# Output weights of the first attention split in the token-major stage, and the last HGRN unit's modulation sums in the places of the HGRN weights

## The chip, the cores and the metric

The kernel runs on one core of a Trainium2 chip, as one launch. The metric is the device time of that launch in microseconds. Everything is computed in float32: TensorE gets each large operand as two parts, a rounded high part and the rest (`hi`, `lo`, here called a split), and multiplies three times (hi·hi, hi·lo, lo·hi).

## The reference

A two-layer diffusion trunk over 1024 latent tokens and 256 context tokens of width 1024. What the change touches lies in layer 0, the even layer. Cut to that:

```
def even_mixer(h_lat, h_ctx, w_in, w_out, ...):
    aq, ak, av, bq, bff, bfb, bi, bg = split(h @ w_in)      # for latent and context tokens
    oa = gqa_axial_attention(...)                            # 8 query heads, 2 key heads
    ob = hgrn2_bidirectional(...)                            # 4 heads, chunked scans both ways
    y  = concat([oa, rms_norm(ob) * silu(bg)]) @ w_out       # 1024 x 1024 output weights
...
mod = silu(c) @ w_mod[l] + b_mod[l]                          # shift, scale, gate for each of two places
x = x + g1 * rms_norm(y, norm_post_mix[l])
```

`w_out` is read from `even_w_out`; `mod` comes from `w_mod`, and its three groups of 2048 columns are summed one after another during layer 0. Neither depends on the tokens' path, so the kernel can place that work where it likes, as long as it is done before its use.

## The kernel before

**Stages.** `even_mixer` first runs `even_token_major`: it normalises and modulates ten tiles of 128 tokens, and multiplies them by the columns of `w_in` for keys and values (kind 0, 256 columns), HGRN inputs (kind 1, 512 columns) and queries (kind 2, 512 columns). A table `plan` lists the products in order, and with each a list of small pieces of other work (`items`: the three pieces K of a key tile, the pieces Q of a query tile, I for the copy-out of an input tile, N for a norm, T and M for transposes and modulation, W for splitting a weight). A product has eight steps of three matmuls; after step k the items with index up to n(k+1)/8 of the list of n are issued. Items are therefore spread evenly, and a longer list moves each of its items to an earlier step. TensorE, ScalarE, VectorE and GpSimd run in exactly this written order (`in_order`); the DMA queue of SyncE (SP) is put in order by the framework's scheduler, with some loads chained among themselves.

Then `hgrn` runs 12 units (4 heads x 3 segments: 256 context tokens, then 512 and 512 latent ones). `chain(u)` is unit u's decay ladder: seven levels m = 1, 2, 4 ... 64, in which VectorE multiplies `hK`, `hQ` and `hT`, ScalarE copies `hKM` (up to m = 16), and TensorE forms small blocks (`h_pd`, from m = 16 on `h_pa`). Between the levels the loop issues matmuls of the next unit's projection (`fill`), the previous unit's end (`side`), one step of the modulation sums (`mods`), and one step of `out_weight`.

**Output weights.** `out_weight(m)`, once in each of the units 3 to 10, loads a 128x1024 piece of `even_w_out` into place `r1`, copies its high part to `r2` on ScalarE (`w_oh`), subtracts on GpSimd (`w_o`), and stores both to the scratch tensor `wod`. In the attention `load_w` fetches the pairs back; the first four go into the weight places `v0h` ... `v3l`, which the HGRN projection has left by then.

**Modulation sums.** `mod_sums` for group 2 runs during the last unit, in which no projection is left to fill TensorE. Each of its eight steps multiplies 128 rows of `w_mod` (two tiles `m_raw`, 512 KB each) into one bank `g_ps`. Its places are `r1`, `r2` and four homes `K2_ij` of the attention's keys, in a pool that begins only where `xh` and `xl`, the projection's inputs, end. Each step reuses the places in turn: six places, so three steps ahead. `begin()` closes the pool of `xh`, opens the attention's pool and starts the attention's first loads; it is called ahead of the last unit.

Of the kernel before, what the change touches and what calls it, by code (L numbers as in the profile page):

```python
# [20 lines left out]
P = 128  # L21
# [47 lines left out]
class Trunk:  # L69
# [148 lines left out]
    def mod_load(self, l, g, k):  # L218
        raws = []
        for i in range(2):  # L220
            of = self.m_tags[self.m_next % len(self.m_tags)]
            raw = of() if callable(of) else self.wp.tile([P, 1024], F32, name="m_raw", tag=of)
            self.m_next += 1
            c0 = 2048 * g + 1024 * i
            self.nc.sync.dma_start(raw, self.a["w_mod"][l, k * P:(k + 1) * P, c0:c0 + 1024])
            raws.append(raw)
        return raws
# [31 lines left out]
            if k == KT - 1:  # L259
                self.mod_finish(l, g, rows, tp, sp)  # L260

    def mod_sums(self, groups, gp, tp, sp, homes):


        self.m_next = 0
        def gate(l, g):
            sl, gi = (slice(64, 128), 1) if 2 * g + 1 == 5 else (slice(0, 64), 0)
            t = sp.tile([P, 2, 512], F32, name="gate_bw", tag="hF", bufs=2)
            self.nc.sync.dma_start(t[sl, 0], self.a["gate_b"][l, gi])
            self.nc.sync.dma_start(t[sl, 1], self.a["gate_w"][l, gi])  # L270
            return t[:, 0], t[:, 1]

        self.m_tags = ["r1", "r2"] + homes
        steps = [(l, g, k) for l, g in groups for k in range(KT)]
# [242 lines left out]
    def even_token_major(self, xh, xl, gps, tp, mp, rp, sp, hg):  # L517
# [149 lines left out]
        with self.in_order(*self.compute):  # L667
# [52 lines left out]
            X_ = [lambda t=t: load_x(t) for t in range(NT)]  # L720
            plan = [(0, 3, [K[0], K[1], K[0], W_[3]]),
                    (1, 0, [W_[4], X_[7], K[1], K[2], W_[5], X_[8], K[0], X_[9], K[2], N[4], K[3]]),
                    (1, 1, [K[1], K[3], N[5], K[2], I[0], N[6], K[3], N[7]]),
# [10 lines left out]
                    (2, 2, [Q[1], Q[0], Q[0], H[1], Q[1]])]  # L734
            plan += [(2, t, [Q[t - 1], Q[t - 2], Q[t - 2]] + [Q[t - 1]]) for t in range(3, 8)]
            plan += [(2, 8, [Q[7], Q[6], Q[6], H[2], Q[7]]), (2, 9, [Q[8], Q[7], Q[7], Q[8]])]
            for i, t, items in plan:
                def hook(k):
                    n = len(items)
                    for f in items[n * k // KT:n * (k + 1) // KT]:  # L740
                        if f:
                            f()
                product(i, t, range(KT), hook)
# [14 lines left out]
    def hgrn(self, xh, xl, gp):  # L758
# [212 lines left out]
                outs = [o for o in outs if next(o, "end") != "end"]  # L971
                yield

        w_out = a["even_w_out"].rearrange("(k p) n -> p k n", p=P)

        def out_weight(m):

            k = 2 * (m % 4)
            raw = self.wp.tile([P, 1024], F32R, name="w_o", tag="r1")
            nc.sync.dma_start(raw.bitcast(F32).rearrange("p (a b) -> p a b", a=2), w_out[:, k:k + 2, 512 * (m // 4):512 * (m // 4) + 512])  # L980
            yield
            yield
            yield
            hi = self.wp.tile([P, 1024], F32R, name="w_oh", tag="r2")
            nc.scalar.copy(hi, raw.bitcast(F32))
            yield
            nc.gpsimd.tensor_tensor(out=raw, in0=raw.bitcast(F32), in1=hi.bitcast(F32), op=OP.subtract)
            yield
            for i, t in enumerate((hi, raw)):
                nc.sync.dma_start(self.wod[m, i].bitcast(F32), t.bitcast(F32))  # L990

        tails = []

        def side():
# [3 lines left out]
        with self.in_order(*self.compute):  # L998
            prepare(3)
            next(mods, None)  # L1000
            for _ in first:
                pass


            for u in range(len(units)):
                last = u + 1 == len(units)
                fill = iter(()) if last else project(u + 1)
                weight = out_weight(u - 3) if 3 <= u < 11 else iter(())
                if last:
                    att, homes = begin()  # L1010
                    next(att)
                    mods = self.mod_sums([(0, 2)], gp, tp, sp, homes)
                    next(mods)
                if u < 8:
                    with self.in_order(mybir.EngineType.SP, behind=True):
                        self.odd_bias_scratch(u)
                x = 0
                for _ in chain(u):
                    side()
                    next(weight, None)  # L1020
                    if x % 3 or last:
                        next(mods, None)
                    for _ in range(3):
                        next(fill, None)
                    side()
                    x += 1
                x = 0
                for _ in fill:
                    x += 1
                    if x % 2 == 0:  # L1030
                        side()
            x = 0
# [75 lines left out]
    def even_attention(self, gp, tp, pp1, sp, more):  # L1108
# [25 lines left out]
        def load_w(m):  # L1134
            pool, tag = (self.wp, f"v{m}") if m < 4 else (more["wp"], f"w{m}")
            W[m] = [pool.tile([P, 1024], F32R, name="w_" + x, tag=tag + x) for x in "hl"]
            for i, t in enumerate(W[m]):
                nc.sync.dma_start(t.bitcast(F32), self.wod[m, i].bitcast(F32))
# [189 lines left out]
        def step(n):  # L1328

            for _ in range(n):  # L1330
# [3 lines left out]
                elif late:  # L1334
# [10 lines left out]
        load_q(2)  # L1345
        load_ctx_keys(1)
        yield
        later = [lambda m=m: load_w(m) for m in range(4)] + [lambda: load_keys(0, 0), lambda: load_keys(0, 1),
                 lambda: load_values(0, NT - 2), lambda: load_keys(1, 0), lambda: load_keys(1, 1)]
        for s in range(N + 8):  # L1350
            pair, half = s // 2, s % 2
            if s < N:
# [1437 lines left out]
    def even_mixer(self):  # L2790
        nc, a, pool = self.nc, self.a, self.pool
        with ExitStack() as es:
# [20 lines left out]
            with ExitStack() as e2:  # L2813
                self.m_tags, self.g_tag = ("r1", "r2"), "hKM"
                sp = pool(e2, "hg", 2, side="right")
                pp = pool(e2, "hg_psum", 1, space=PSUM)
                mods = self.mod_bursts([(0, 1)], tp, sp)

                def begin():
                    eh.close()  # L2820
                    at = self.at = Homes(pool(es, "at0", 2), None, ("l_p", "a_ph1", "a_pl1", "gate", "y"))
                    homes = [lambda t=f"K2_{i}{j}": at.first.tile([P, 1024], F32, name="m_raw", tag=t, bufs=1)
                             for i in range(2) for j in range(2)]
                    return self.even_attention(gp, tp, pp, at, more), homes
# [139 lines left out]

# [6 lines left out]
```

## Time and profile before

| what | us |
|---|---|
| median of 3 runs (lowest, highest) | 3281.98 (3278.56, 3282.49) |
| the profiled execution | 3279.68 |
| its span | 3277.6 |
| DVE busy, POOL busy in the span | 2159.5, 1592.6 |
| first and last copy `w_oh` on ScalarE | 340.0, 567.2 |
| first and last modulation matmul of the last unit | 592.2, 617.8 |

The span runs from the first to the last recorded instruction; the profiled execution lasted 2.1 us longer than its span and was 2.3 us shorter than the median. PE is TensorE, PEld its weight loads, ACT ScalarE, DVE VectorE, POOL GpSimd, SP or SPq the DMA queue that SyncE issues. A row of the timeline gives start, duration, engine, line, operation, output and inputs, and in brackets the time for which the engine had sat idle before it and what ended that. A row of the waits gives the sum, the number of times, and the longest. A row of stretches gives busy times by engine, the clock that TensorE was granted, and the DMA engines' busy share and GB/s.

### The profile page before, as it was taken

To read this page: it belongs to the slowest core of one execution; us is meant where nothing else is said; L and a number is where in the kernel's file an instruction comes from. 1 tells how busy PE (TensorE), PEld (TensorE's weight loads), DVE (VectorE), ACT (ScalarE), POOL (GpSimd) and SP (SyncE) were. 2 spreads that over 40 slices of the span, in tenths; PEclk is the share of its full clock that TensorE was granted. 3 is DMA by queue.
4 is the path that set the end of the run, shared out by engine and by line. 5 is a ranking of instruction groups with operands and counts; after the bars stand their busy time and mean duration, and the time that the engine had idled before them with its cause. 6 is when DMAs were issued, how large, how long until landed. Compare 5 with 4: busy or idle time off the path is not lost.

```text
span 3277.6 us, 48744 instructions
## 1 busy us (share of the span) xinstructions
PE 3076.2 (94%) x18161; PEld 2545.1 (78%) x18161; DVE 2159.5 (66%) x3603; ACT 1506.7 (46%) x2697; POOL 1592.6 (49%) x1173
## 2 busy tenths in 40 slices
PE   7989999789998899999999989999998989999999
PEld 4867777578886688888888768899986758888787
DVE  4456666577775788888678662477775465555687
ACT  3323333366665434433444442566665543343444
POOL 1130222287774677777500111677775367777300
PEclk8999999899999899999999989999998989999999
DMA  7333222621114244443375672222224212222755
GB/s 252 105 102 112 87 89 75 229 87 63 58 48 162 82 152 147 142 145 137 137 249 200 226 227 107 74 63 62 61 73 162 91 64 84 77 88 84 249 193 189
DMA packets 214709, 412.91 MB, mean 126 GB/s; under 512 B 25392, under 2 KB 87360, under 8 KB 214472
## 3 DMA queue, kind: packets, MB, share of 16 engines
q1 hardware_dynamic: 204776, 376.24, 34.2%
q0 software_dynamic: 9696, 33.57, 2.6%
q8 instruction: 142, 2.33, 0.3%
q14 instruction: 95, 0.78, 0.1%
HBM read 322.67 MB, written 87.44 MB: 125 GB/s over the span
## 4 chain that ended last, share of the span: by engine, by line
PE 76%; DVE 12%; DMA 4%; ACT 3%; issue 3%; POOL 2%; SPq 0%; POOLq 0%; ACTq 0%; DVEq 0%
PE g_ps L140 21%; PE u_g L140 13%; PE d_ps L140 11%; PE u_v L140 10%; PE u_pc L140 3%; PE a_pv L140 2%; PE c_pv L140 2%; PE c_s L140 2%; PE c_pt L2593 2%; PE a_pt L1210 2%; DMA m_raw<-in_w_mod 1%; DVE a_pl L1212 1%; PE o_ps L140 1%; PE a_s L140 1%; DMA d_rawB<-in_w_down 1%
## 5 line engine op out<-in xcount | busy, mean ns | idle before, releaser
L148 POOL TENSOR_TENSOR rs_r<-rs_e,mhalf 128x1 f32<-128x1 f32 (+3 forms) x102 | 82.4, 809 | 788.3 <-DVE rs_e L147 370.3
L140 PE MATMUL d_ps<-d_Bl,d_Ah 128*128 128x512 f32 x704 | 277.3, 394 | 3.4 <-DVE d_Bl L1976 2.9
L140 PE MATMUL d_ps<-d_Bh,d_Ah 128*128 128x512 f32 x704 | 276.6, 393 | 3.8 <-ACT d_Bh L1975 2.0
L2576 POOL TENSOR_SCALAR c_p<-c_p,rl 128x640 f32<-128x640 f32 (+1 forms) x128 | 232.8, 1820 | 94.2 <-DVE rl L2575 62.4
L140 PE MATMUL d_ps<-d_Bh,d_Al 128*128 128x512 f32 x704 | 276.2, 392 | 0.7 <-DVE d_Al L1976 0.6
L140 PE MATMUL g_ps<-xh,w_hi 128*128 128x512 f32 (+1 forms) x640 | 259.7, 406 | 5.6 <-DVE hq L805 3.5
L1190 POOL TENSOR_SCALAR l_p<-l_p,rl 128x1280 f32<-128x1280 f32 x64 | 225.4, 3521 | 54.9 <-DVE rl L1189 49.0
L140 PE MATMUL g_ps<-xh,w_lo 128*128 128x512 f32 (+1 forms) x640 | 240.2, 375 | 1.6 <-POOL w_lo L2476 1.6
L140 PE MATMUL g_ps<-xl,w_hi 128*128 128x512 f32 (+1 forms) x640 | 240.4, 376 | 0.0
L1212 DVE TENSOR_TENSOR a_pl<-a_pt,a_ph 128x512 fp32r<-128x512 f32 (+1 forms) x200 | 118.9, 602 | 87.0 <-ACT a_ph L1211 86.6
L366 DVE CUSTOM_DVE_ANT_0 m_raw<-m_raw,c_row 128x512 f32<-128x512 f32 x128 | 149.7, 1180 | 24.9 <-DMA m_raw<-in_w_mod 24.6
L1651 DVE TENSOR_TENSOR f_u<-u_v,f_p 128x512 f32<-128x512 f32 x88 | 60.4, 687 | 158.8 <-PE u_v L140 158.8
L140 PEld LDWEIGHTS d_ps<-d_Bl,d_Ah 128*128 128x128 f32 x704 | 133.2, 189 | 34.8 <-DVE d_Bl L1976 6.8
L140 PEld LDWEIGHTS d_ps<-d_Bh,d_Ah 128*128 128x128 f32 x704 | 133.3, 189 | 33.7 <-ACT d_Bh L1975 3.6
L1637 POOL TENSOR_TENSOR w_S4l<-w_s,w_S4h 128x512 fp32r<-128x512 f32 x44 | 57.1, 1298 | 208.2 <-ACT w_S4h L1636 208.2
L140 PEld LDWEIGHTS d_ps<-d_Bh,d_Al 128*128 128x128 f32 x704 | 133.4, 189 | 29.3 <-DVE d_Al L1976 1.7
L1211 ACT CAST a_ph<-a_pt 128x512 fp32r<-128x512 f32 (+1 forms) x200 | 101.8, 517 | 109.1 <-PE a_pt L1210 109.1
L2596 DVE TENSOR_TENSOR c_pl<-c_pt,c_ph 128x256 fp32r<-128x256 f32 (+1 forms) x256 | 112.9, 469 | 58.5 <-ACT c_ph L2595 57.3
L140 PE MATMUL g_ps<-w_hi,xh 128*128 128x512 f32 (+1 forms) x368 | 142.8, 388 | 5.5 <-DVE xh L2350 2.9
L140 PEld LDWEIGHTS g_ps<-xh,w_hi 128*128 128x128 f32 x640 | 123.8, 193 | 25.0 <-issue 7.6
L140 PEld LDWEIGHTS g_ps<-xh,w_lo 128*128 128x128 f32 x640 | 123.3, 193 | 24.7 <-POOL w_lo L2476 2.0
L140 PE MATMUL g_ps<-w_lo,xh 128*128 128x512 f32 (+1 forms) x368 | 137.6, 374 | 4.0 <-DVE w_lo L2337 2.9
(602 smaller groups left out, 10026.3 us busy)
## 6 DMA issues: line engine op xcount, KB each, us to landing
w_raw<-in_w_up SPq DMA_DIRECT2D x88, 512.0 KB
d_rawA<-actd SPq DMA_DIRECT2D x77, 512.0 KB
d_rawB<-in_w_down SPq DMA_DIRECT2D x74, 512.0 KB
m_raw<-in_w_mod SPq DMA_DIRECT2D x128, 256.0 KB
m_raw<-in_w_mod SPq DMA_DIRECT2D x48, 512.0 KB
actd<-f_t SPq DMA_DIRECT2D x22, 640.0 KB
actd<-f_t SPq DMA_DIRECT2D x22, 512.0 KB
vcd<-cv_st POOLq DMA_DIRECT2D x20, 512.0 KB, 2.9
```

Source lines behind the costliest of these rows:

```text
L140: return self.nc.tensor.matmul(out, lhsT, rhs, start=start, stop=stop, skip_group_check=True, **k)
L148: nc.gpsimd.tensor_tensor(out=r[:p, :n], in0=e[:p, :n], in1=self.mhalf[:p, :n], op=OP.pow)
L366: nc.vector.tensor_tensor_reduce(out=w, in0=w, in1=halves[1][n % 2], scale=1.0, scalar=0.0, op0=OP.mult, op1=OP.add, accum_out=acc[:, k, o ...
L1190: nc.gpsimd.tensor_scalar(Pt[:, :nk], Pt[:, :nk], rl, None, op0=OP.mult)
L1210: nc.tensor.transpose(pt[:, m, qt * P:(qt + 1) * P], Pt[:, kts[j + m] * P:(kts[j + m] + 1) * P], self.ident)
L1211: nc.scalar.copy(ph[:, j:j + n], pt[:, :n])
L1212: nc.vector.tensor_tensor(out=pl[:, j:j + n], in0=pt[:, :n], in1=ph[:, j:j + n].bitcast(F32), op=OP.subtract)
L1637: nc.gpsimd.tensor_tensor(out=lo, in0=part(j, name), in1=hi.bitcast(F32), op=OP.subtract)
L1651: nc.vector.tensor_tensor(out=out, in0=x, in1=y, op=OP.add)
L2576: nc.gpsimd.tensor_scalar(Pt[:, :n], Pt[:, :n], rl, None, op0=OP.mult)
L2593: nc.tensor.transpose(pt[:, j, :], Pt[:, (src + j) * P:(src + j + 1) * P], self.ident)
L2596: nc.vector.tensor_tensor(out=vap(pl, o, dims), in0=pt[:, :cnt], in1=vap(ph, o, dims).bitcast(F32), op=OP.subtract)
```

## The change

- Each product from plan entry 3 on gets extra items: `out_load(m)` loads a 128x512 piece (256 KB) of `even_w_out` into the low place of one of three new pairs `o0` to `o2`, `out_split(m)`, two entries later, copies the high part on ScalarE and subtracts in place on VectorE, and `out_store(m)` stores both halves to `wod`. There are 16 pieces. `out_weight` in the HGRN loop is gone.
- `mod_sums` takes as places `r1`, `r2` and the eight weight places `v0h` ... `v3l`: ten, so five steps ahead. The homes in the attention's pool are gone.
- `begin()` is called after the third level of the last unit, with the sums already going.
- The attention's deferred loads `later` fetch keys and values first, and the four pairs of output weights after them.
- The scratch for the descriptors of GpSimd's DMAs is halved.

```diff
-        self.m_tags = ["r1", "r2"] + homes
+        self.m_tags = ["r1", "r2"] + [f"v{i}{x}" for i in range(4) for x in "hl"]
...
+            def out_load(m):
+                k, c0 = m % 8, 512 * (m // 8)
+                O[m] = [self.wb.tile([P, 512], F32R, name="w_o" + x, tag=f"o{m % 3}{x}") for x in "hl"]
+                with self.chained():
+                    nc.sync.dma_start(O[m][1].bitcast(F32), w_out[:, k, c0:c0 + 512])
+
+            def out_split(m):
+                hi, lo = O[m]
+                nc.scalar.copy(hi, lo.bitcast(F32))
+                nc.vector.tensor_tensor(out=lo, in0=lo.bitcast(F32), in1=hi.bitcast(F32), op=OP.subtract)
+
+            def out_store(m):
+                c = 512 * (m % 2)
+                for i, t in enumerate(O.pop(m)):
+                    nc.sync.dma_start(self.wod[m // 2, i][:, c:c + 512].bitcast(F32), t.bitcast(F32))
...
+            for m in range(16):
+                at = 3 + 3 * m // 4
+                plan[at][2].append(lambda m=m: out_load(m))
+                plan[at + 2][2].extend((lambda m=m: out_split(m), lambda m=m: out_store(m)))
...
-        def out_weight(m):
...
-            nc.scalar.copy(hi, raw.bitcast(F32))
-            yield
-            nc.gpsimd.tensor_tensor(out=raw, in0=raw.bitcast(F32), in1=hi.bitcast(F32), op=OP.subtract)
...
                 if last:
-                    att, homes = begin()
-                    next(att)
-                    mods = self.mod_sums([(0, 2)], gp, tp, sp, homes)
+                    mods = self.mod_sums([(0, 2)], gp, tp, sp)
                     next(mods)
...
                     x += 1
+                    if last and x == 3:
+                        att = begin()
+                        next(att)
...
-        later = [lambda m=m: load_w(m) for m in range(4)] + [lambda: load_keys(0, 0), ...
+        later = [lambda: load_keys(0, 0), ... + [lambda m=m: load_w(m) for m in range(4)]
...
-    nc = bacc.Bacc("TRN2", target_bir_lowering=False, num_devices=1, dynamic_dma_scratch_size=8192)
+    nc = bacc.Bacc("TRN2", target_bir_lowering=False, num_devices=1, dynamic_dma_scratch_size=4096)
```

VectorE in the token-major stage, around the products (0, 4) to (0, 6), before: the norm of a token tile (`n_x`), the value part of a key tile (`v_st`) and its rotation (`qk_n` to `qk_r`) follow one another directly.

```order
L147 TENSOR_SCALAR rs_e<-ms 128x1
L615 TENSOR_SCALAR n_x<-n_x,rs_r 128x1024
L527 TENSOR_TENSOR v_st<-g_ps,v_st 128x2x64
L454 TENSOR_REDUCE qk_ms<-qk_sq 128x2
L147 TENSOR_SCALAR rs_e<-qk_ms 128x2
L147 TENSOR_SCALAR rs_e<-ms 128x1
L615 TENSOR_SCALAR n_x<-n_x,rs_r 128x1024
L459 TENSOR_TENSOR qk_n<-g_ps,rs_r 128x128
```

The same place of VectorE after the change; `w_ol` is the low half of a piece of the output weights.

```order
L147 TENSOR_SCALAR rs_e<-ms 128x1
L614 TENSOR_SCALAR n_x<-n_x,rs_r 128x1024
L731 TENSOR_TENSOR w_ol<-w_ol,w_oh 128x512 x2
L526 TENSOR_TENSOR v_st<-g_ps,v_st 128x2x64
L453 TENSOR_REDUCE qk_ms<-qk_sq 128x2
L147 TENSOR_SCALAR rs_e<-qk_ms 128x2
L147 TENSOR_SCALAR rs_e<-ms 128x1
L614 TENSOR_SCALAR n_x<-n_x,rs_r 128x1024
L731 TENSOR_TENSOR w_ol<-w_ol,w_oh 128x512
L458 TENSOR_TENSOR qk_n<-g_ps,rs_r 128x128
```

Three subtractions now stand ahead of the rotation of this key tile, two of them ahead of its value part.

GpSimd in the HGRN units 4 and 5, before: the subtraction `w_o` stands between the unit's outputs (`h_o`, stored to `hgd`) and the copy `hqb`.

```order
L148 TENSOR_TENSOR rs_r<-rs_e,mhalf 128x2
L1096 TENSOR_SCALAR h_dg<-ident,rs_r 128x128 x2
L1103 TENSOR_TENSOR h_o<-h_o,hgate 128x256
L1105 DMA hgd<-h_o 128x256
L987 TENSOR_TENSOR w_o<-w_o,w_oh 128x1024
L934 COPY hqb<-hQ 128x512
L987 TENSOR_TENSOR w_o<-w_o,w_oh 128x1024
L148 TENSOR_TENSOR rs_r<-rs_e,mhalf 128x4
```

The same place after.

```order
L148 TENSOR_TENSOR rs_r<-rs_e,mhalf 128x2
L1098 TENSOR_SCALAR h_dg<-ident,rs_r 128x128 x2
L1105 TENSOR_TENSOR h_o<-h_o,hgate 128x256
L1107 DMA hgd<-h_o 128x256
L955 COPY hqb<-hQ 128x512
L148 TENSOR_TENSOR rs_r<-rs_e,mhalf 128x4
```

All eight such subtractions have left GpSimd.

The DMA queue of SP around the last unit, before: `w_h` and `w_l` are fetched output weights, `K_`, `V_` and `a_q` the attention's keys, values and queries.

```order
L1138 DMA w_h<-wod 128x1024
L1144 DMA K_0c<-k2d 128x2x256
L1124 DMA a_q<-q2d 128x256 x2
L1156 DMA V_8_5947<-v2d 128x2x256
L1124 DMA a_q<-q2d 128x256
L1144 DMA K_1c<-k2d 128x2x256
L225 DMA m_raw<-in_w_mod 128x1024 x14
L1138 DMA w_l<-wod 128x1024
L1150 DMA K_00_6373<-k2d 128x1024
```

The same place after; two more `m_raw`, for `r1` and `r2`, stand far ahead of these rows, at the HGRN unit 4.

```order
L224 DMA m_raw<-in_w_mod 128x1024 x3
L268 DMA gate_bw<-in_gate_b 64x512
L269 DMA gate_bw<-in_gate_w 64x512
L224 DMA m_raw<-in_w_mod 128x1024 x11
L1146 DMA K_0c<-k2d 128x2x256
L1126 DMA a_q<-q2d 128x256 x2
L1158 DMA V_8_6131<-v2d 128x2x256
L1126 DMA a_q<-q2d 128x256
L1146 DMA K_1c<-k2d 128x2x256
L1152 DMA K_00_6323<-k2d 128x1024
```

Before, 14 of the 16 modulation tiles are asked for after everything else that the last unit and the attention's first block need; after, all are asked for ahead of that, and the fetches of the output weights have moved behind the keys.

More of the change, by code (lines that the diff above doesn't have):

```diff
@@ L220, in mod_load @@
         for i in range(2):
-            of = self.m_tags[self.m_next % len(self.m_tags)]
-            raw = of() if callable(of) else self.wp.tile([P, 1024], F32, name="m_raw", tag=of)
+            raw = self.wp.tile([P, 1024], F32, name="m_raw", tag=self.m_tags[self.m_next % len(self.m_tags)])
             self.m_next += 1
@@ L260, in mod_bursts, with mod_sums @@
                 self.mod_finish(l, g, rows, tp, sp)
-    def mod_sums(self, groups, gp, tp, sp, homes):
+    def mod_sums(self, groups, gp, tp, sp):
         self.m_next = 0
@@ L720, in even_token_major @@
             X_ = [lambda t=t: load_x(t) for t in range(NT)]
+            w_out, O = a["even_w_out"].rearrange("(k p) n -> p k n", p=P), {}
+            def out_load(m):
[11 more added lines that the diff above has]
+                    nc.sync.dma_start(self.wod[m // 2, i][:, c:c + 512].bitcast(F32), t.bitcast(F32))
             plan = [(0, 3, [K[0], K[1], K[0], W_[3]]),
@@ L972, in tail @@
                 yield
-        w_out = a["even_w_out"].rearrange("(k p) n -> p k n", p=P)
-        def out_weight(m):
-            k = 2 * (m % 4)
-            raw = self.wp.tile([P, 1024], F32R, name="w_o", tag="r1")
-            nc.sync.dma_start(raw.bitcast(F32).rearrange("p (a b) -> p a b", a=2), w_out[:, k:k + 2, 512 * (m // 4):512 * (m // 4) + 512])
-            yield
-            yield
-            yield
-            hi = self.wp.tile([P, 1024], F32R, name="w_oh", tag="r2")
-            nc.scalar.copy(hi, raw.bitcast(F32))
[L986 to L990, printed above, removed]
         tails = []
@@ L1007, in hgrn @@
                 fill = iter(()) if last else project(u + 1)
-                weight = out_weight(u - 3) if 3 <= u < 11 else iter(())
                 if last:
-                    att, homes = begin()
-                    next(att)
-                    mods = self.mod_sums([(0, 2)], gp, tp, sp, homes)
+                    mods = self.mod_sums([(0, 2)], gp, tp, sp)
                     next(mods)
@@ L1019, in hgrn @@
                     side()
-                    next(weight, None)
                     if x % 3 or last:
@@ L1347, in even_attention @@
         yield
-        later = [lambda m=m: load_w(m) for m in range(4)] + [lambda: load_keys(0, 0), lambda: load_keys(0, 1),
-                 lambda: load_values(0, NT - 2), lambda: load_keys(1, 0), lambda: load_keys(1, 1)]
+        later = [lambda: load_keys(0, 0), lambda: load_keys(0, 1), lambda: load_values(0, NT - 2), lambda: load_keys(1, 0),
+                 lambda: load_keys(1, 1)] + [lambda m=m: load_w(m) for m in range(4)]
         for s in range(N + 8):
@@ L2821, in begin @@
                     at = self.at = Homes(pool(es, "at0", 2), None, ("l_p", "a_ph1", "a_pl1", "gate", "y"))
-                    homes = [lambda t=f"K2_{i}{j}": at.first.tile([P, 1024], F32, name="m_raw", tag=t, bufs=1)
-                             for i in range(2) for j in range(2)]
-                    return self.even_attention(gp, tp, pp, at, more), homes
+                    return self.even_attention(gp, tp, pp, at, more)
                 try:
```

## The prediction

> **What bounds the kernel now.** I read the page first (span, busy shares, the chain that ended last), then stretches by stage, then TensorE's waits in each stage, then timelines around those waits.
>
> ```profile
> span 3277.6 us, 48744 instructions
> PE 76%; DVE 12%; DMA 4%; ACT 3%; issue 3%; POOL 2%; SPq 0%; POOLq 0%; ACTq 0%; DVEq 0%
> 70.00:222.00 152.00, 138.89 (x734) 114.33 (x734) 84.64 (x161) 53.73 (x94) 43.91 (x32) 1.00 0.33 101
> 222.00:592.00 370.00, 344.97 (x3823) 274.61 (x3824) 241.98 (x483) 115.64 (x212) 70.65 (x74) 0.97 0.30 100
> 592.00:622.00 30.00, 22.23 (x332) 9.83 (x330) 17.81 (x36) 5.35 (x9) 0.00 (x0) 0.89 0.94 350
> ```
>
> Three quarters of the chain is TensorE (PE), so a wait of PE is time, and what runs beside a busy PE is free. The stretches (PE, PEld, DVE, ACT, POOL, then clock, DMA share, GB/s) are the token-major stage once its products run, the HGRN units up to the last projection, and the last unit with its modulation sums. Only the third is bound by the DMA engines (share 0.94), and PE has most to gain per microsecond there. PE's waits, in the second and the third stretch:
>
> ```profile
> PE h_pa L140 <- DVE hQ L891: 11.1, 6, 2.4
> ...
> PE g_ps L140 <- DMA m_raw<-in_w_mod: 6.9, 7, 5.2
> ```
>
> **HGRN units: eight GpSimd subtractions leave.** The first of those waits is no weakness of the ladder itself:
>
> ```profile
> 372.97 0.68 DVE L891 TENSOR_TENSOR hQ<-hQ,hT 128x512 f32<-128x512 f32 x1
> 375.67 3.40 DVE L891 TENSOR_TENSOR hQ<-hQ,hT 128x512 f32<-128x512 f32 x1
> 376.14 2.36 POOL L987 TENSOR_TENSOR w_o<-w_o,w_oh 128x1024 fp32r<-128x1024 f32 x1
> 379.21 0.46 PE L140 MATMUL h_pa<-hQ,hKM 128*32 128x32 f32 x32 [2.43 <-DVE hQ L891]
> 408.23 2.84 DVE L891 TENSOR_TENSOR hQ<-hQ,hT 128x512 f32<-128x512 f32 x1
> 411.22 0.46 PE L140 MATMUL h_pa<-hQ,hKM 128*32 128x32 f32 x32 [2.34 <-DVE hQ L891]
> 574.01 0.46 PE L140 MATMUL h_pa<-hQ,hKM 128*32 128x32 f32 x32 [1.41 <-DVE hQ L891]
> 347.54 2.57 POOL L987 TENSOR_TENSOR w_o<-w_o,w_oh 128x1024 fp32r<-128x1024 f32 x1
> 347.89 2.25 DVE L892 TENSOR_TENSOR hT<-hT 128x16 f32<-128x16 f32 x1
> ```
>
> The same VectorE instruction takes 0.68 us alone and 3.40 or 2.84 us beside the GpSimd subtraction `w_o`, and then PE waits. Five of the eight subtractions end in such a wait: two like 379.21, two like 411.22, and 574.01. The sixth wait in the row is the rest (11.1 - 2 x 2.43 - 2 x 2.34 - 1.41 = 0.15 us). In the three units of 256 tokens the slowed one is a small `hT` (row 347.89), while PE has the next projection of 512 tokens to do, and no wait follows. Without `w_o`, hQ ends 3.40 - 0.68 = 2.72 us earlier (all of a 2.43 wait goes) or 2.84 - 0.68 = 2.16 us earlier (2.16 of 2.34 go), and in the last case all of 1.41: 2 x 2.43 + 2 x 2.16 + 1.41 = **10.6 us gained**. What is late next is `hKM` on ScalarE, which loses the copy `w_oh` from its queue as well. Above, the gain is bounded by the whole row, 11.1; below, I put half, 5, if the ladder meets PE again one level later. I take 10.6.
>
> [...]
>
> **Last unit: modulation tiles come earlier.** Now:
>
> ```profile
> 593.58 16.55 SPq L225 DMA_DIRECT2D m_raw<-in_w_mod  x14
> 595.00:600.00 5.00, 0.25 (x2) 0.19 (x4) 1.57 (x3) 0.77 (x2) 0.00 (x0) 0.64 1.02 365
> 599.75 2.35 PE L140 MATMUL g_ps<-m_raw,csil 128*32 128x512 f32 x6 [5.22 <-DMA m_raw<-in_w_mod]
> 593.75 0.68 DVE L889 TENSOR_TENSOR hK<-hK,hF 128x512 f32<-128x512 f32 x1
> 603.40 0.69 DVE L891 TENSOR_TENSOR hQ<-hQ,hT 128x512 f32<-128x512 f32 x1 [6.73 <-PE h_pd L140]
> 605.27 0.68 DVE L891 TENSOR_TENSOR hQ<-hQ,hT 128x512 f32<-128x512 f32 x1
> 615.48 0.69 DVE L889 TENSOR_TENSOR hK<-hK,hT 128x512 f32<-128x512 f32 x1 [1.38 <-PE h_pa L140]
> 618.29 1.09 PE L908 MATMUL h_kt<-ident,hK 128*128 128x128 f32 x8
> ```
>
> All tiles but two are issued at 593.58 or later, when `xh` is given up. PE waits 5.22 us for the second step, and after it runs at the pace of the loads (1 MB a step at 365 GB/s and more: 2.5 to 2.9 us). Since the ladder's blocks stand behind the sums in PE's order, VectorE waits too (6.73 us). The ladder goes from its first `hK` (593.75) to its last (615.48) in 21.73 us, six level steps. After the change, the first five steps' ten tiles have places before the unit's first sum. These are the places that the output weights used, and the queue filled them here, as PE let them go, between
>
> ```profile
> 565.94 0.33 SPq L1138 DMA_DIRECT2D w_h<-wod  x1
> 590.29 0.32 SPq L1138 DMA_DIRECT2D w_h<-wod  x1
> ```
>
> so the tiles are asked for then. The last three steps follow as the first three free their places. Then nothing but VectorE, ScalarE and PE in turn sets the pace: 605.27 - 603.40 = 1.87 us a level where the data was there. The last two levels have PE between hK and hQ (row 615.48 waited for it); I add 0.25 for each and get 6 x 1.87 + 2 x 0.25 = 11.7 instead of 21.73 us: **10.0 us gained**. The transposes `h_kt` (618.29) follow the ladder by the same distance. Bounds: 6.9, PE's DMA waits alone, and 10.5, without the 0.25. What moved behind the tiles is not needed so soon:
>
> ```profile
> L140 PE MATMUL g_ps<-K_0c,a_q x16: 278/365/1202, 622.4 to 641.2; 128*128 128x256 f32 x16
> L140 PE MATMUL a_s<-K,a_q x256: 387/397/501, 656.6 to 982.7; 128*128 128x512 f32 x128
> L140 PE MATMUL g_ps<-w_h,a_oh x160: 393/478/483, 690.7 to 1036.9; 128*128 128x512 f32 x160
> ```
>
> The first keys are used at 622.4, some 612 after the gain. They are issued once the third step has freed its place, near 600, and the output weights have until about 680. If that cover were gone, each 512 KB of the four pairs would cost 1.4 us.
>
> **Token-major stage: what comes in.** 16 loads, 16 copies, 16 subtractions, 32 stores. Prices, from equal or equally wide instructions:
>
> ```profile
> 77.57 0.69 DVE L631 TENSOR_TENSOR xl<-n_t,xh 128x512 fp32r<-128x512 f32 x1
> 108.91 0.59 ACT L571 COPY b_st<-g_ps 128x512 f32<-128x512 f32 x1
> 97.08 0.43 DVE L487 TENSOR_TENSOR qk_r<-qk,qk 128x256 f32<-128x256 f32 x1 [0.35 <-POOL qk L483]
> 98.53 0.38 PE L537 MATMUL k_pt<-ident,qk_r 128*128 128x128 f32 x2
> 104.03 0.43 DVE L487 TENSOR_TENSOR qk_r<-qk,qk 128x256 f32<-128x256 f32 x1 [0.35 <-POOL qk L483]
> 104.93 0.38 PE L537 MATMUL k_pt<-ident,qk_r 128*128 128x128 f32 x2
> 139.01 0.41 PE L537 MATMUL k_pt<-ident,qk_r 128*128 128x128 f32 x2 [0.63 <-DVE qk_r L475]
> 75.93 0.33 PE L623 MATMUL n_pt<-ident,n_x 128*128 128x128 f32 x1 [1.90 <-DVE n_x L615]
> 1150.16 5.43 SPq L351 DMA_DIRECT2D m_raw<-in_w_mod  x4
> 1152.62 0.90 DVE L366 CUSTOM_DVE_ANT_0 m_raw<-m_raw,c_row 128x512 f32<-128x512 f32 x1 [0.79 <-DMA m_raw<-in_w_mod]
> ```
>
> All on the path they would cost 16 x (0.69 + 0.59) = 20.5 us; the stretch has room (VectorE 84.64 of 152 us, ScalarE 53.73), so most is hidden behind PE's products. What isn't are transposes in PE's order whose input now comes later. Key tile 4: its rotation ends at 97.51, its transposes start at 98.53, 1.0 us of slack; three subtractions stand ahead (1.9 us, as VectorE starts one every 0.62): 0.9 us. Key tile 6: slack 0.5 us, again three subtractions since (1.9), its transposes two steps earlier in a longer list (2 x 0.7), less the 0.9 by which PE is late already: 1.9. The transposes of tiles 4 to 7, which already wait 1.90 us for `n_x`, are asked for one step earlier: 0.7. Context transposes that wait for one of three banks, their copies on ScalarE being behind: between 0 and 2, I take 1. The wait at 139.01 goes (-0.6). Sum: **4 us lost**. Below, the bound is -0.6, all else hidden; above, 20.5.
>
> The pieces themselves come in time: a 256 KB load can be used 1152.62 - 1150.16 = 2.5 us after its issue. A place goes round in store 2.5, load 2.5, copy 0.6, subtraction 0.7, some queueing: about 7 us for three pieces, and 13 pieces after the first three want 30 us of the 50 in which they run. The SP queue is held by stores that wait for the two engines; behind them stand the last two `w_in` loads, needed some 5 us after their landing. The other edits (scratch halved, loads in another order) cost nothing while GpSimd's DMAs are as few as here.
>
> **Sum.** 3279.7 for the profiled execution - 10.6 - 10.0 + 4 = 3263.1; the median of the runs lies 2.3 higher, so **3265 us**. A change under 0.2% (6.6 us) can't be told from none in this kernel.
>
> **Rivals.**
> - [...] Chance 0.16.
> - The last unit gains only 4, as a tile still comes late or the first softmax, bound by other engines, gives time back: 3271. For it: SP takes its queue in order, and `gate_bw` stands among the tiles. Chance 0.12.
> - The change doesn't do what it says to the ladder: hQ is late for another reason (the copies of hKM), and 5 of 10.6 come: 3271. Against it: row 372.97. Chance 0.06.
> - Slower: the places' round trip becomes the stage's pace. The 13 pieces are 4.3 rounds; it decides where a round takes over (50 + 21) / 4.3 = 16.5 us, 2.4 times what the rows give. At 19 us the rounds take 82, 32 more than the 50, in place of the 4: 3265 - 4 + 32 = 3293. For it: every piece needs two trips and an in-order queue. Chance 0.04.
> - My forecast, 3260 to 3270: 0.62.
>
> Faster by over 0.2% (under 3275.4) are the forecast, most of the first rival and all of the next two: 0.62 + 0.10 + 0.12 + 0.05 = 0.89, of which I take 0.03 off for what I haven't seen: 0.86. Same 0.10, slower 0.04. The range reaches from the forecast with all upper bounds, 3259, to the first rival's middle and a little more, 3275.
>
> **What would show it.** No hQ over 1 us in the HGRN stretch, and PE's wait for hQ there under 1 us. No PE wait for `m_raw` in the last unit, its ladder in 11 to 13 us. PE waits for `qk_r` and for the context transposes of 3 to 5 us between 70 and 150. It is wrong if PE waits there by 10 us and more behind ScalarE copies that wait for a load of `w_o`, or if the modulation sums still pace the ladder.

## The result and the profile after

The changed kernel took 3260.97 us (median of 6 runs, 3258.97 to 3269.73) against 3282.06 us before: 0.994 of the time, 95% interval 0.9927 to 0.9953. Timed again beside later kernels it gave 0.9959 (0.9944 to 0.9974). The forecast was 3265, and the range 3259 to 3275 holds the result. As will be seen, the gains came from where the forecast had put them, but that the sum came out right was partly luck: two of its terms were too small, one on each side, and a third was put at nothing.

The page's first line and its chain, after:

```profile
span 3257.1 us, 48812 instructions
PE 76%; DVE 11%; issue 4%; ACT 3%; DMA 3%; POOL 2%; SPq 0%; POOLq 0%; ACTq 0%; DVEq 0%
```

TensorE still bounds the kernel. TensorE's waits in the token-major stage and the start of the HGRN units (70 to 236 us), then in the HGRN units up to the last (236 to 584 us):

```profile
PE g_ps L140 <- DVE hq L826: 6.6, 1, 6.6
PE q_pt L556 <- DVE qk_r L486: 5.5, 7, 1.2
PE k_pt L536 <- DVE qk_r L486: 3.8, 2, 2.0
PE n_pt L622 <- DVE n_x L614: 2.5, 2, 1.9
...
PE h_po L140 <- DVE hS L1056: 7.3, 6, 1.8
PE h_kt L929 <- ACT hkt L935: 2.7, 2, 1.9
...
PE h_pa L140 <- DVE hQ L912: 0.5, 3, 0.2
```

The wait for hQ, 11.1 us before, is 0.5. New are 3.8 us for the rotated keys `qk_r`, which was expected, and 6.6 us instead of 3.5 for `hq`, which was not.

The four places in the program that divide the changed stretch are the first and last `hK` of the ladder (its rows `hK<-hK,hT`), the first modulation matmul of the last unit, and the first `a_s` of the attention. Rows of the tiles, before and then after (minimum, median and maximum ns, then first and last start):

```profile
L889 DVE TENSOR_TENSOR hK<-hK,hT x72: 411/691/855, 233.8 to 615.5; 128x512 f32<-128x512 f32 x48, 128x256 f32<-128x256 f32 x24
L140 PE MATMUL g_ps<-m_raw,csil x64: 592/617/1062, 592.2 to 617.8; 128*32 128x512 f32 x64
```

```profile
L910 DVE TENSOR_TENSOR hK<-hK,hT x72: 408/691/905, 242.5 to 597.5; 128x512 f32<-128x512 f32 x48, 128x256 f32<-128x256 f32 x24
L140 PE MATMUL g_ps<-m_raw,csil x64: 591/593/617, 584.5 to 597.9; 128*32 128x512 f32 x64
L140 PE MATMUL a_s<-K,a_q x256: 387/397/501, 640.1 to 966.2; 128*128 128x512 f32 x128
```

The first `hK` comes 8.7 us later, the first modulation matmul of the last unit 7.7 us earlier, the last `hK` 18.0 earlier and `a_s` 16.5 earlier (656.6 before). Between these marks, in every kernel that was run (us; token-major counts from the first `k_pt`, which itself scatters between 58.0 and 60.2):

| kernel | token-major | HGRN units | last unit | to first a_s | ratio to before (95%) |
|---|---|---|---|---|---|
| before | 174.4 | 358.4 | 23.3 | 41.1 | |
| changed | 182.3 | 342.0 | 13.0 | 42.6 | 0.994 (0.9927 to 0.9953) |
| changed, again (a0) | 184.5 | 341.6 | 13.0 | 42.3 | 0.9959 (0.9944 to 0.9974) |
| e1, no subtraction | 173.5 | 343.8 | 24.0 | 40.9 | 0.9958 (0.9944 to 0.9973) |
| e2, sums alone | 173.7 | 356.6 | 14.8 | 44.2 | 0.9981 (0.9972 to 0.999) |
| e3, pieces alone | 181.8 | 341.9 | 24.3 | 40.5 | 0.9978 (0.997 to 0.9987) |
| e4, scratch alone | 175.3 | 355.0 | 24.5 | 42.7 | 1.0007 (0.9998 to 1.0016) |
| e5, e2 with six places | 172.7 | 356.7 | 20.8 | 43.1 | 0.9989 (0.998 to 0.9998) |
| e6, hq moved | 181.0 | 343.2 | 13.0 | 42.6 | 0.9946 (0.9934 to 0.9958) |
| e7, pieces later | 178.6 | 341.4 | 15.1 | 44.1 | 0.9941 (0.9927 to 0.9954) |
| e8, e6 and e7 | 176.8 | 341.2 | 15.9 | 44.2 | 0.994 (0.9928 to 0.9952) |
| e9, DVE subtracts | 173.9 | 343.7 | 24.7 | 43.1 | 0.9962 (0.9948 to 0.9976) |
| e10, e8 repeated in effect | 175.7 | 341.2 | 13.0 | 43.3 | 0.9925 (0.991 to 0.994) |
| e11, end of sums later | 177.5 | 342.9 | 15.9 | 39.5 | 0.9927 (0.9912 to 0.9942) |

Behind the last `a_s` the kernels are alike and still take 2291 to 2301 us in these profiles, with no order in it. So the stage lengths tell mechanisms apart that the total time alone cannot.

### The profile page after: what moved, and what is told of

The parts are those of the page before. It is cut to its first block, busy times and chain, and to the rows that moved or that the text cites. A ratio compares the mean times of both kernels' runs of the same rounds, so it can differ in the third digit from the quotient of the medians.

```text
span 3257.1 us, 48812 instructions
## 1 busy us (share of the span) xinstructions
PE 3065.0 (94%) x18161; PEld 2538.8 (78%) x18161; DVE 2147.4 (66%) x3619; ACT 1508.0 (46%) x2705; POOL 1576.6 (48%) x1165
## 3 DMA queue, kind: packets, MB, share of 16 engines
q8 instruction: 143, 2.34, 0.3%
## 4 chain that ended last, share of the span: by engine, by line
PE 76%; DVE 11%; issue 4%; ACT 3%; DMA 3%; POOL 2%; SPq 0%; POOLq 0%; ACTq 0%; DVEq 0%
PE g_ps L140 20%; PE u_g L140 14%; PE d_ps L140 12%; PE u_v L140 10%; PE u_pc L140 3%; PE a_pv L140 2%; PE c_pv L140 2%; PE c_s L140 2%; PE c_pt L2595 2%; PE a_pt L1212 2%; DVE a_pl L1214 1%; PE o_ps L140 1%; PE a_s L140 1%; DMA d_rawB<-in_w_down 1%; ACT a_ph L1213 1%
## 5 line engine op out<-in xcount | busy, mean ns | idle before, releaser
L2597 ACT CAST c_ph<-c_pt 128x256 fp32r<-128x256 f32 (+1 forms) x256 | 98.4, 414 | 91.4 <-PE c_pt L2595 89.2
```

The source lines that it names most:

```text
L2597: nc.scalar.copy(vap(ph, o, dims), pt[:, :cnt])
```

## The experiments

**The HGRN units: subtraction or something else (e1, e9).**

```diff
-            nc.gpsimd.tensor_tensor(out=raw, in0=raw.bitcast(F32), in1=hi.bitcast(F32), op=OP.subtract)
+            # e1: left out;  e9: nc.vector.tensor_tensor(... the same ...)
```

> The kernel before, with the GpSimd subtraction of the output weights left out (their low halves are stored as loaded); loads, copies and stores stay. [...] Then every hQ takes 0.7 us, PE's waits for hQ sum to under 1 us (11.1 before), the clock dips at 410, 476 and 510 go, and the stretch from the first hK of the HGRN units to the first modulation matmul of the last unit shrinks from 358.4 us to about 343: 3267 us. Rival 1, hQ is late for ScalarE's copies: waits and stretch stay, 3282. Rival 2, the dips of the clock have nothing to do with the stalls: the waits go but the dips stay, stretch 348, 3271.

> The kernel before with the subtraction of the output weights on VectorE instead of GpSimd, all else as before. [...] Rival: the ladder waits for room on VectorE just as well: 1.2 us more on it is 8 x 1.2 = 10 us of waits, stretch 358, 3281.

Taking away nothing but the subtraction gives all of the HGRN gain: 343.8 us, waits for hQ 0.5. Since e1 keeps them, neither the copies `w_oh` nor the loads and stores mattered. With the subtraction on VectorE the stretch is 343.7, and the waits for hQ are 2.1 us. Rows of VectorE from e9:

```profile
374.79 1.22 DVE L987 TENSOR_TENSOR w_o<-w_o,w_oh 128x1024 fp32r<-128x1024 f32 x1
375.93 0.69 DVE L889 TENSOR_TENSOR hK<-hK,hT 128x512 f32<-128x512 f32 x1
376.53 0.69 DVE L891 TENSOR_TENSOR hQ<-hQ,hT 128x512 f32<-128x512 f32 x1
```

The same 128x1024 subtraction takes 1.22 us here against 2.36 on GpSimd, and the hQ that follows takes 0.69 and not 3.40. What hurts is GpSimd working beside VectorE, not the load on VectorE. I had expected 346 to 349 us, with some 4 us of waits for hQ; it cost less, presumably since VectorE mostly had that 1.2 us to spare. One changed word in the kernel before gives 0.9962, where the whole change gave 0.994 and 0.9959.

**The clock behind a stall.** Rival 2 of e1 (clock dips that have nothing to do with the stalls) fell as well: in e1 and e9, without the long waits, the dips near 411, 476 and 510 are gone too. In the kernel before, windows around the stall that ends at 411.22 (the third last column is the granted clock):

```profile
410.00:412.00 2.00, 0.78 (x35) 0.77 (x36) 1.86 (x3) 0.00 (x0) 0.53 (x1) 1.00 0.44 178
412.00:414.00 2.00, 2.00 (x40) 1.78 (x39) 0.93 (x3) 0.66 (x2) 0.00 (x0) 0.51 0.36 141
414.00:416.00 2.00, 2.00 (x23) 1.80 (x14) 1.47 (x3) 0.00 (x0) 0.00 (x0) 0.64 0.64 239
416.00:418.00 2.00, 2.00 (x29) 1.93 (x29) 1.32 (x3) 0.07 (x1) 0.00 (x0) 1.00 0.06 24
```

After the wait, TensorE runs at half clock: 2 x (1 - 0.51) + 2 x (1 - 0.64) = 1.7 us lost, on top of the 2.34 waited. The loss comes in portions: every stretch of low clock between 60 and 700 us in all profiles loses 1.7, 3.4 or 5.1 us, that is half of 3.4 us, or of two or three times 3.4. The kernel before has four such portions in its HGRN units (6.8 us), the changed one none, and e2 and e4, which keep the subtraction, three and two: their HGRN stretches of 356.6 and 355.0 are 1.8 and 3.4 us under the 358.4. The same stretch as a whole, before and changed, has a granted clock of 0.98 and 1.00:

```profile
233.80:592.20 358.40, 333.37 (x3727) 264.39 (x3727) 239.56 (x476) 113.08 (x205) 70.65 (x74) 0.98 0.30 100
```

```profile
242.50:584.50 342.00, 327.23 (x3727) 259.26 (x3727) 220.32 (x475) 105.53 (x197) 51.40 (x66) 1.00 0.21 68
```

Over the four profiles with the GpSimd subtraction in place (before, e2, e4, e5), 16 waits of 2.31 to 2.43 us were followed by half clock 10 times: always near 410 and 475, twice of four near 508, never near 378. The 1.93 us wait for `hkt` near 290 was followed by it in 5 of 14 profiles, the 1.76 us waits for `hS` in these units in none of 42.

Why half clock never follows the wait near 378, and what sets the length of a portion, no run shows.

**The two parts alone (e2, e3) and the whole again (a0).** e2 is the kernel before with `mod_sums`, `begin` and `later` of the change; e3 is the change with these three as before.

> The kernel before with the second part of the change alone: modulation sums in the weight places, begin after the third level, keys ahead of the fetched output weights; the output weights stay in the HGRN units and the scratch at 8192. Theory: the HGRN stretch stays at 358 us; from the first modulation matmul of the last unit to the last hK 13 us instead of 23.3; of the 10 gained some 3 are given back in the first softmax, where PE waits for hS and runs at half clock: 3275. Rival 1, the sums gain only where the output weights have left the places and the queue: 17 us and more for the last unit, 3279 or above. Rival 2, nothing is given back: 3272.

> The change's first part alone: output weights in 16 pieces in the token-major stage, scratch 4096; modulation sums, begin and the order of the late loads as before. Theory: first hK of the HGRN units 8 us later than before (242 against 233.8), stretch from there to the first modulation matmul 342 us against 358.4, last unit as before (23 us): 3274. Rival: the 8 us of the token-major stage come in part from the places of the modulation tiles, then the first hK is under 240: 3270.

> The changed kernel itself, timed again beside the next three. Its two parts alone gave 0.9981 and 0.9978 of the time before, together 0.9959; the whole gave 0.994. Theory: the parts add up (in the traces the first a_s of the attention comes 7.9, 8.7 and 17.3 us earlier, counted from the first k_pt), and the rest of the gap is scatter of the stages behind them (2291 to 2299 us from the last a_s to the end): 0.9945 to 0.996. Rival: the parts help each other in the last unit: 0.994 or less again, with a shorter attention.

Both parts gain, and each where it should: e3 has the HGRN gain and the token-major loss, with the last unit as before; e2 has the last unit's gain alone. They add up: 0.9981 x 0.9978 = 0.9959, the value that the whole gave on its second timing. To the first `a_s`, counted from the first `k_pt`, they gain 7.9 and 8.7 us, and the whole 17.3 in its first profile and 15.8 in its second. No effect between them is needed; that 0.994 was lower is within its scatter.

**Early places or many (e5).** In e2, six places instead of ten:

```diff
-        self.m_tags = ["r1", "r2"] + [f"v{i}{x}" for i in range(4) for x in "hl"]
+        self.m_tags = ["r1", "r2"] + [f"v{i}{x}" for i in range(2) for x in "hl"]
```

> The run of the second part alone (modulation sums in the weight places), but with six places (r1, r2, v0h to v1l) instead of ten, so three steps ahead as before the change; all else as there. It tells early places from many places. Theory: both are needed. The first three steps come early and PE does not wait for the second (5.2 us before), but the last five steps need places that the earlier ones give up one by one: 1 MB at some 370 GB/s each, 2.8 us a step, so that from the first modulation matmul to the last hK it takes 17 to 19 us, between the 23.3 of before and the 14.8 with ten places. Rival 1, early is enough: 13 to 15 us. Rival 2, ten places are what counts: 22 us and more.

The last unit takes 20.8 us: more than the 17 to 19 expected, less than the 22 of the rival, and much nearer to 23.3 than to 14.8. Rows of TensorE from e5:

```profile
589.30 1.07 PE L140 MATMUL g_ps<-m_raw,csil 128*32 128x512 f32 x8
605.86 1.05 PE L140 MATMUL g_ps<-m_raw,csil 128*32 128x512 f32 x4 [1.79 <-DMA m_raw<-in_w_mod]
607.12 1.84 PE L140 MATMUL g_ps<-m_raw,csil 128*32 128x512 f32 x4 [0.21 <-DMA m_raw<-in_w_mod]
```

The second step no longer waits, but the loads set the pace from the fourth on. Early places alone move the wait to the end of the unit; what counts is that ten and not six of the 16 tiles have places before the unit begins.

**hq and the halved scratch (e4, e6).** The change halves the scratch to 4096 bytes so that the new pairs fit. e4 is the kernel before with that number alone; e6 is the changed kernel with one small tile taken later.

```diff
-        ones = sp.tile([P, P], F32, name="ones", bufs=1)
-        nc.vector.memset(ones, 1.0)
 ...
             for _ in first:
                 pass
+            ones = sp.tile([P, P], F32, name="ones", bufs=1)
+            nc.vector.memset(ones, 1.0)
```

> The kernel before with nothing but the scratch for GpSimd's DMA descriptors halved (8192 to 4096). Theory: all tiles that are placed from the left move down by 4096 bytes, so that hq of the first HGRN unit now shares its last 64 bytes with the second place of q_st, and VectorE has to wait for the last store of q_st: DVE waits some 3.3 us at hq, PE's wait for hq grows from 3.5 to 6.6 us: 3285. Rival: the scratch serves only DMA descriptors, and the 3.1 us at hq in the changed kernel come from the SP queue, which its pieces have made late: no change, 3282, with a wait of 3.5.

> The changed kernel with the tile ones (512 bytes) taken from the pool after the first projection instead of ahead of it, so that hsig and hq of the first unit lie 512 bytes lower and hq no longer touches the second place of q_st. Theory: VectorE's wait for the last store of q_st at hq (3.3 us) goes, PE's wait for hq falls from 6.6 to 3.5 us, and the first hK comes 2 to 3 us earlier against q_pt: 3258. Rival, the SP queue's lateness holds hq in another way: the wait stays 6.6, 3261.

VectorE and TensorE at the first `hq`, in the kernel before, the changed one, e4 and e6, in this order:

```profile
221.32 0.42 DVE L805 SCALAR_TENSOR_TENSOR hq<-g_ps,hsig 128x256 f32<-128x256 f32 x1 [0.17 <-ACT hsig L801]
221.80 0.58 PE L140 MATMUL g_ps<-xh,w_hi 128*128 128x256 f32 x1 [3.49 <-DVE hq L805]
```

```profile
217.58 10.20 SPq L564 DMA_DIRECT2D q2d<-q_st  x3
230.81 0.42 DVE L826 SCALAR_TENSOR_TENSOR hq<-g_ps,hsig 128x256 f32<-128x256 f32 x1 [3.31 <-DMA q2d<-q_st]
231.28 0.58 PE L140 MATMUL g_ps<-xh,w_hi 128*128 128x256 f32 x1 [6.63 <-DVE hq L826]
```

```profile
222.21 0.43 DVE L805 SCALAR_TENSOR_TENSOR hq<-g_ps,hsig 128x256 f32<-128x256 f32 x1 [3.33 <-DMA q2d<-q_st]
222.69 0.58 PE L140 MATMUL g_ps<-xh,w_hi 128*128 128x256 f32 x1 [6.66 <-DVE hq L805]
```

```profile
228.67 0.42 DVE L826 SCALAR_TENSOR_TENSOR hq<-g_ps,hsig 128x256 f32<-128x256 f32 x1 [0.31 <-ACT hsig L822]
229.15 0.58 PE L140 MATMUL g_ps<-xh,w_hi 128*128 128x256 f32 x1 [3.49 <-DVE hq L826]
```

The scratch alone makes VectorE wait for the last store of `q_st`, and moving `hq` down by 512 bytes takes that away. The tiles of the token-major stage are placed from the left of SBUF, behind the scratch; those of the HGRN units are placed from the right. When the left ones slid by 4096 bytes, the second place of `q_st` (bytes 110272 to 114368 of a partition in the built program) came to share 64 bytes with `hq` (108288 to 110336), and `hq` then waits for that place's last reader, the store (3.31 and 3.33 us in the rows above, 0.17 and 0.31 where the two don't touch it so late). Before, the same 64 bytes lay in the first place (110272 to 114368 then), whose last store comes one query tile earlier, so the overlap as such was not new. From the last `q_pt` to the first `hK` it takes 15.8 us in e6 as before, 18.1 in the changed kernel and 17.7 in e4: 2 us. The totals show this less clearly (e4 1.0007, e6 0.9946 against 0.9959, all intervals overlapping).

**Where the pieces stand (e7, e8).** Nine splits stay where nine stood, from (1, 5) on; the other seven go into the query products, away from the key tiles 4 to 7:

```diff
+                at = (10, 11, 11, 12, 13, 14, 14, 15, 16)[m] if m < 9 else m + 11
+                extra.setdefault((at - 2, 7), []).append(lambda m=m: out_load(m))
...
+                    extra.setdefault((at, 2), []).append(lambda m=m: out_high(m))
+                    extra.setdefault((at, 4), []).extend((lambda m=m: out_low(m), lambda m=m: out_store(m)))
```

> The changed kernel with other places for the 16 pieces: none in the products from (0, 4) to (1, 4), nine splits in (1, 5) to (1, 9) where they stood already, seven in the query products (2, 3) to (2, 9), one each, with the copy after the step 2 and the subtraction after the step 4, between qk_r and q_st. Theory: the waits of 1.8 and 2.0 us for qk_r at the key tiles 4 and 6, and the half-clock stretch of 1.7 us behind the second, came from the subtractions ahead of the rotation; they go, the query tiles have 2 us of VectorE idle there, and the first hK comes 5 us earlier: 3256. Rival, the query tiles have no slack (PE waits 0.5 us for qk_r in each already): 0.7 us more for each of seven, 3261.

> Both edits of the two runs before this together. Theory: they add up, 7 to 8 us less than the changed kernel: 3253. Rival: with the pieces in the query products, their stores stand ahead of the last q_st stores in the SP queue and hold up hF and hq again: 3257.

In the changed kernel, VectorE and TensorE at key tile 4, key tile 6, and the clock behind it:

```profile
98.60 0.68 DVE L731 TENSOR_TENSOR w_ol<-w_ol,w_oh 128x512 fp32r<-128x512 f32 x1
99.20 0.28 DVE L458 TENSOR_TENSOR qk_n<-g_ps,rs_r 128x128 f32<-128x128 f32 x1
100.15 0.42 DVE L486 TENSOR_TENSOR qk_r<-qk,qk 128x256 f32<-128x256 f32 x1 [0.35 <-POOL qk L482]
100.72 0.41 PE L536 MATMUL k_pt<-ident,qk_r 128*128 128x128 f32 x2 [1.81 <-DVE qk_r L486]
...
108.93 0.63 PE L536 MATMUL k_pt<-ident,qk_r 128*128 128x128 f32 x2 [2.02 <-DVE qk_r L486]
...
110.00:112.00 2.00, 2.00 (x7) 1.50 (x7) 1.33 (x4) 0.56 (x1) 1.24 (x2) 0.50 0.73 251
```

In e7 the wait at the key tiles is 0.2 us and this stretch of half clock is gone. Another of 1.7 us stands near 76 instead, behind the wait for `n_x`, as in e8, e10, e11 and the second profile of the changed kernel. So the stage has as many portions as in the changed kernel, and what e7 gains there is mostly the waits. The query tiles' waits grow from 5.5 to 6.4 us for seven pieces. From the first `k_pt` to the first `q_pt` it takes 99.3 us against 98.8 before and 104.3 to 106.3 in the changed kernel. e8 adds e6's gain: token-major 176.8 us. But 2 to 3 us of this are missing behind it, in the last unit: TensorE stood still there in the middle of a block of 32 matmuls, in e2, e7, e8 and e11 (1.9, 2.2, 3.0 and 2.2 us), and not in the changed kernel or e10. From e8, and its instruction queue q8 over the whole span (packets, MB, share of the 16 engines):

```profile
588.25 0.22 PE L140 MATMUL h_pa<-hQ,hKM 128*32 128x32 f32 x1 [2.98 <-issue]
...
q8 instruction: 143, 2.34, 0.3%
```

"issue" means that no semaphore explains it. The DMA engines are full at that time (share 0.98 to 1.01). What TensorE lacked the traces don't show; my estimate, from the packets of q8, is that it was its own instructions. In every profile this queue moves 142 or 143 packets of 16 KB, of the kind "instruction", which is one for some 256 matmuls and weight loads (2 x 18161 of these over 142 packets in the kernel before). The four stops all come at the same place in TensorE's order, ahead of its matmul or weight load 10177 or 10178, counted from the start. Just there a packet of q8 lands late (in e2, e7, e8 and e11 at 599.84, 588.43, 587.02 and 589.95), and TensorE goes on 1.2 to 1.5 us behind it. In the other four profiles with ten places the same packet had landed 2.2 us or more before TensorE came to that place. No run moved that packet, and why it came late stays open.

**The first softmax (e10, e11).** 1.5 us of the last unit's gain are given back before the first `a_s`, up to 3 in e2, e7 and e8. I suspected the end of the sums, 1.7 us of `mod` and `gate_bw` on VectorE ahead of the states `hS`.

> The last combination (hq out of the way, pieces away from the key tiles) with one more edit: the end of the modulation sums (transposes, the sums of mod and gate_bw on VectorE, 1.7 us) is issued six steps later, behind the states hS of the last unit. Theory: of the last unit's gain some 3 us are given back because these four VectorE pieces stand ahead of hS when the ladder ends; PE's wait for hS falls from 3.3 to about 1.6 us, and half-clock stretches behind it get fewer: from the last hK to the first a_s 41 to 43 us instead of 44.2. Rival: VectorE is the bound in the first softmax, and the pieces cost the same where they now stand: 44 us, with the wait moved to a later place.

> The run before this left VectorE's order as it was, since the end of the sums was issued by the ladder's own loop; here that loop holds it back as well, and it stands behind all states hS of the last unit. Theory: the 1.7 us of mod and gate_bw stood ahead of hS; PE's wait for hS falls from 3.3 to 1.6 us or less and at most one half-clock stretch behind it stays: 40 to 42.5 us from the last hK to the first a_s (43.3 and 44.2 in the two runs before, 41.1 in the kernel before the change), 3255. Rival, hS waits for ScalarE's second copy hds as much as for VectorE: wait 2.5 us or more, 43 to 44 us, 3257.

e10's edit, in the loop after the last ladder, came too late: the ladder's own loop had issued the end of the sums, and VectorE's order was e8's. e10 is thus a second sample of e8, without the "issue" gap. e11 holds the sums back in both loops:

```diff
-                    if x % 3 or last:
+                    if x < 9 if last else x % 3:
                         next(mods, None)
...
+                if x > 5:
                     next(mods, None)
```

TensorE's wait for `hS` between 584 and 650 us, in e10 and in e11:

```profile
PE h_po L140 <- DVE hS L1068: 3.3, 1, 3.3
```

```profile
PE h_po L140 <- DVE hS L1068: 1.5, 1, 1.5
```

The stage takes 39.5 us instead of 43.3 and 44.2, less even than before the change (41.1). In time e11 is at 0.9927 and e10 at 0.9925; the "issue" gap and one clock portion eat the difference. Both are below the changed kernel's second timing with intervals that do not meet, and overlap its first. The best that can be said is 0.1 to 0.3% on top of the change.

## Why the prediction was right, step by step

- **HGRN units, 10.6 us forecast, 16.4 measured.** The waits were right: TensorE's waits between 236 us and the last unit fell by 10.5 us (24.1 to 13.6), nearly all of it hQ's. What the sum lacked is the clock: four portions of 1.7 us (with the waits 17.3, 0.9 more than the stretch shows; the fourth portion, near 290, comes and goes without the change). The rows for it were in the profile before (clock 0.97 in the HGRN stretch), and I did not ask what had lowered it. e1 and e9 show the cause by two different edits.
- **Last unit, 10.0 forecast, 10.3 measured** (23.3 to 13.0), with no wait for `m_raw` left and the ladder at VectorE's and TensorE's pace; e5 shows that six places were not enough. The rival in which a tile still comes late did not come. Its other half, the softmax giving time back, did: 1.5 us, by the order on VectorE (e11) and half clock behind the wait.
- **Token-major stage, 4 lost forecast, 7.9 measured** (10.1 in the second profile). Key tile 6 cost 2.0 (1.9 forecast), the `n_x` transposes 0.65 (0.7), the wait at 139 went (-0.6). Key tile 4 cost 1.8 and not 0.9, and the banks of the context transposes nothing. The two missing terms are one clock portion (1.7) and `hq` (3.1 of wait, 2 in the end). The failing step is the sentence that the scratch costs nothing: I looked at what the scratch serves and not at what lies behind it in memory.
- **The first rival, 13 us lost instead of 4 (3274, chance 0.16, and the range's upper end with it):** no run shows the 9 us that it adds; 7.9 us were lost, by the waits, the clock and `hq` as above. VectorE's and GpSimd's instructions did meet, but none of VectorE's 16 subtractions was slowed (0.683 to 0.695 us each); three of GpSimd's were. Of the eight `rs_r` of 128x2 on GpSimd, the three that began 0.06 to 0.13 us behind a subtraction took 1.12 to 1.17 us; the five others, and all eight before, took 0.69 to 0.70. Three rows of the changed kernel:

```profile
101.63 0.69 DVE L731 TENSOR_TENSOR w_ol<-w_ol,w_oh 128x512 fp32r<-128x512 f32 x1
...
101.75 1.13 POOL L148 TENSOR_TENSOR rs_r<-rs_e,mhalf 128x2 f32<-128x2 f32 x1 [1.64 <-DVE rs_e L147]
...
109.99 0.69 POOL L148 TENSOR_TENSOR rs_r<-rs_e,mhalf 128x2 f32<-128x2 f32 x1 [1.58 <-DVE rs_e L147]
```

  VectorE waited 0.26 us for one of the three, and TensorE for none of them. Here the instruction that began second took longer. Not so in the HGRN units before: hQ at 375.67 began 0.47 us ahead of the GpSimd subtraction at 376.14, and it was hQ that took 3.40 us, while the subtraction took 2.36. What decides which of the two is slowed, the runs don't show. In the query tiles GpSimd's pieces take up to 2.6 us, but no subtraction stood beside those.
- **Places as the stage's pace:** VectorE waited 6.9 us in all for the copies `w_oh`, and ScalarE 0.9 us for a load or a place; TensorE waited for none of the 16 pieces directly.

The sum: -16.4 - 10.3 + 7.9 + 1.5, and 0.8 for a first `k_pt` that came later in this profile, is -16.5 us at the first `a_s`, against -16.6 forecast. The missed clock (-6.8 and +1.7) and the missed `hq`, key tile 4 and softmax (2 to 3, 0.9 and 1.5) cancelled almost, which is luck and not reckoning. The other 4 us of the two spans come from behind the last `a_s` (2294.9 and 2290.9 us), inside that part's scatter of 2291 to 2301.

## What to carry to other kernels

A stall of TensorE is priced by its wait and by the clock behind it: where the rows show half clock after such a wait, add the portion (at 411 here, 1.7 us on a wait of 2.34), and take it off again when the wait goes. Work that is moved off the path of one stage is paid for in the next by whatever stands behind it in order there (here 7.9 us lost for 16.4 gained), so put it where the engine's own row shows it idle, and not evenly (in e7, 99.3 us from the first `k_pt` to the first `q_pt` instead of 104.3 to 106.3). When a buffer's size changes, compare where the neighbours of every later stage now lie, and who uses shared bytes last: 64 of them were worth a wait of 3.3 us.

## What the runs showed of the hardware

- A GpSimd subtraction of 128x1024 beside VectorE's 128x512 multiplication takes 2.36 us and stretches the latter from 0.7 to 2.8 or 3.4; the same subtraction on VectorE takes 1.22 us, so here GpSimd did not relieve VectorE but held it up, by 2.16 or 2.72 us, for longer than the work is worth.
- TensorE's granted clock fell by half in portions of 3.4 us (1.7 us lost in each), in the HGRN units after waits of 2.3 to 2.4 us in 10 of 16 cases, and after the waits of 1.76 us for `hS` in none of 42.
- TensorE stood still for 1.9 to 3.0 us inside a block of 32 equal matmuls, with no semaphore that explains it, in four profiles out of eight with early modulation tiles and ten places. In these four, a 16 KB packet of the instruction queue q8 landed only 1.2 to 1.5 us before TensorE went on; in the other four it had landed 2.2 us or more before TensorE came there.
- A GpSimd instruction that began some 0.1 us behind a VectorE subtraction took 1.12 to 1.17 us instead of 0.69, three times out of three, and the subtraction took no longer than alone.
